# Which engine makes the low halves of the weights, and how a row of token factors is spread over the partitions

## The chip, the core and the metric

The kernel runs on one core of a Trainium2 chip. The metric is the device time of one execution in microseconds (us), the median of several runs. The engines are TensorE (PE, its weight loads shown apart as PEld), VectorE (DVE), ScalarE (ACT), GpSimd (POOL) and SyncE (SP, which issues most DMAs).

## What is computed

A decoder trunk of two layers on 512 tokens of width 1024, in float32. The first layer mixes with a gated delta rule (8 heads of 128), the second with forgetting attention (16 heads of 64). Each layer then has a gated feed-forward part (SwiGLU, inner width 2816).

```python
def swiglu(h, w_in, w_out):
    gu = h @ w_in
    return (jax.nn.silu(gu[..., :D_FF]) * gu[..., D_FF:]) @ w_out
...
    for layer in range(DEPTH):
        h = rms_norm(x, pre_mix_norm[layer])
        ...
        x = x + rms_norm(mix, post_mix_norm[layer])
        f = swiglu(rms_norm(x, pre_ffn_norm[layer]), w_ffn_in[layer], w_ffn_out[layer])
        x = x + rms_norm(f, post_ffn_norm[layer])
    return x
```

`mix` is the delta rule, or attention on shared keys and values. `rms_norm` divides each token by the root of the mean of its squares, so every norm needs one factor per token.

## The kernel before, in words

**Tiling.** The residual is kept transposed: features on the partitions, 8 tiles of 128 features, 512 tokens along the free dimension. A unit of weights is 128 output features by 1024 input features.

**Split products.** To keep float32 accuracy, every weight and every activation is split into a high half (rounded to fp32r) and a low half (the remainder). A product takes three passes per block of 128 inputs: high by high, low by high, high by low (`product`). A unit therefore costs 24 passes of 512 columns on PE. Its halves are made by `halve`: ACT copies the loaded tile `wf` into `wh`, then DVE or POOL subtracts, `wl = wf - wh`. Each of `wf`, `wh` and `wl` has four buffers.

**Who subtracts.** `next_halves` decides for each unit, from the planner's clocks: `late` is how far DVE's planned work reaches beyond PE's present time. In the kernel before, POOL gets the unit when `late` is over 1.0 us and either the unit is not yet wanted or POOL would be done sooner.

**The order of the work.** Nothing runs while the program text is executed: the calls on `PE`, `DVE`, `ACT`, `POOL` and `SP` are recorded with a planned cost (`Plan.cost`, `Plan.note`), by generators (`main`, `gates`, `k_post`, `inverse`, `recurrence`, `boundary`, ...) that a small planner resumes. Afterwards `ordered` and `listed` make four rounds of list scheduling over all recorded groups and keep the best. Each engine then executes its own list strictly in that order. So a decision in one place can move instructions everywhere; in the trace all recorded instructions bear the line of the recording helper (L102), and tiles tell them apart.

**Stages.** First come the normalised input (tiles `b`) and the units of k and z. Beside them, `gates` makes the decay matrices: a series on 32 columns (tiles `sp`) on DVE, then per head two products with `SLR` into bank `mid` and an exponential on ACT. `k_post` (per head: three convolution steps on DVE, SiLU on ACT, column sums into bank `sm`, four 128x128 products into `mid`) leads to the head's matrix; `inverse` inverts all of them in 31 steps on DVE; `merge` and `recurrence` follow. Then out projection, the first boundary, the feed-forward part, the second boundary, attention, the third boundary, the second feed-forward part, and the finish.

**A boundary** (`boundary`, `first_units`, `token_rsqrt`) leads from one sublayer to the next, in two halves of 256 tokens. The output tiles are scaled (tiles `b`), added to the residual (tiles `a`, three of four on POOL), and split into the next operand (tiles `h`: high by ACT, low by DVE) for eight feature tiles in turn. PE's first products of the next sublayer, into banks `ob` and `prj`, take one feature tile after the other as they come.

**The token factor** (`token_rsqrt`, lines 712 to 726) sums squares over features by products with a column of ones into `sm` (128 tokens per column), DVE scales them (`tokr`), POOL raises them to the power -1/2 (`tokn`, `tokp`), and for each chunk of 128 tokens a product of the broadcast column with the identity puts the row of factors on all partitions, in bank `mid`. There are 15 such calls with 32 chunks: one of four chunks at the start, and 14 of two chunks.

Of the kernel before, what the change touches and what calls it, by code (L numbers as in the profile page):

```python
# [17 lines left out]
P = 128  # L18
# [406 lines left out]
def trunk(  # L425
# [21 lines left out]
    plan = Plan()  # L447
    PE, DVE, ACT, POOL, SP = (
        plan.engine(e, n)
        for e, n in ((nc.tensor, "PE"), (nc.vector, "DVE"), (nc.scalar, "ACT"), (nc.gpsimd, "POOL"), (nc.sync, "SP"))  # L450
    )
# [35 lines left out]
    def small(shape, tag, bufs, dt=F32):  # L487
        return plan.tile(tag, bufs, spool, shape, dt, nm(tag))
# [7 lines left out]
    def mid():  # L496
        return bank("mid", 2)

    def sm():
        return bank("sm", 2)  # L500
# [7 lines left out]
    def ck(c, n=P):  # L508
        return slice(c * n, (c + 1) * n)
# [3 lines left out]
    ident, U = (cst_sb[:, i] for i in range(2))  # L513
# [28 lines left out]
    def signal(name, after=0.0):  # L542
        signals[name] = max(plan.now(), current[0][5], plan.finish)
# [51 lines left out]
    used = [0]  # L595
# [11 lines left out]
    def halve(pieces=1, act=ACT, dve=None):  # L607
        i = len(ready)
        _, n, eng, cols, thin = seq[i]
        t = landed[i]  # L610
        hi = plan.tile("wh", 4, wpool, [P, KT, P], F32R, nm("wh"))
        if not thin:
            lo = plan.tile("wl", 4, wpool, [P, KT, P], F32R, nm("wl"))
            ready.append((hi[:, :, :cols], lo[:, :, :cols]))
        else:

            lo = hi[:, :, cols:]
            ready.append(hi[:, :, : 2 * cols])
        landed[i] = None
        left[i] = n * T  # L620
        index[hi.tensor.name] = i
        step = n // pieces

        def piece(k):
            a, h, l = (w[:, k : k + step, :cols] for w in (t, hi, lo))
            act.activation(h, a, AF.Copy)
            (dve or eng).tensor_tensor(out=l, in0=a, in1=f(h), op=ALU.subtract)

        return [lambda k=k: piece(k) for k in range(0, n, step)]
# [3 lines left out]
    def landing():  # L633
        while len(landed) < min(used[0] + 5, len(ready) + 4, len(seq)):
            for go in land():
                go()

    def next_halves():

        i = len(ready)  # L640
        landing()
        late = plan.free["DVE"] - plan.now()
        slow = late > 1.0 and (used[0] < i or late + 1.2 > 2.4 + plan.free["POOL"] - plan.now())
        for go in halve(dve=POOL if slow else DVE):
            go()
        landing()
        signal(f"half{i}")

    def halver():
        while len(ready) < len(seq):  # L650
            i = len(ready)
            if i > 3:
                yield (f"left{i - 4}",)
            yield (lambda: 0.0 if used[0] >= i else min(plan.free["DVE"], plan.free["POOL"]) - 0.4,)
            if len(ready) == i:
                next_halves()
# [4 lines left out]
    def unit():  # L661
        i = used[0]
        used[0] += 1
        while len(ready) <= i:
            next_halves()
        landing()
        return ready[i]
# [40 lines left out]
    def token_sums(ps, src, chunks):  # L708
        for c in chunks:
            PE.matmul(ps[:, c : c + 1], lhsT=src[:, ck(c)], rhs=ones[:, 0:1], start=True, stop=True)  # L710

    def token_rsqrt(acc, tok, r, use):

        cs = range(tok.start // P, tok.stop // P)
        sl = slice(cs[0], cs[-1] + 1)
        yield ("#sm", plan.ready(acc[:, tok]))
        ps = sm()
        token_sums(ps, acc, cs)
        m = small([P, NC], "tokr", 4)
        DVE.tensor_scalar(out=m[:, sl], in0=ps[:, sl], scalar1=1.0 / D, scalar2=EPS, op0=ALU.mult, op1=ALU.add)  # L720
        POOL.tensor_tensor(out=r[:, sl], in0=m[:, sl], in1=mhalf[:, sl], op=ALU.pow)
        yield ("done", "#mid")
        ps = mid()
        for c in cs:
            PE.matmul(ps[:, ck(c)], lhsT=r[:, c : c + 1].broadcast_to([P, P]), rhs=ident, start=True, stop=True)
        use(ps[:, tok])

    def halves_of(x, k, sets, hs, tok, act=ACT, dve=DVE):
# [5 lines left out]
    class Norm:  # L734
# [7 lines left out]
        def factor(self, i, tok):  # L742
            def use(ps):
                ACT.activation(self.rs[:, tok], ps, AF.Copy)

            yield from token_rsqrt(self.acc, tok, self.r, use)
            signal(f"{self.name}.rs{i}")

    def finish(x, mix, acc, g, tok):

        r = small([P, NC], "tokp", 2)
        banks = []
        yield from token_rsqrt(acc, tok, r, banks.append)
        for k in range(KT):
            m, xk = mix[k][:, tok], x[k][:, tok]
            DVE.scalar_tensor_tensor(out=m, in0=m, scalar=gain(g, k), in1=banks[0], op0=ALU.mult, op1=ALU.mult)
            (POOL if k % 2 else DVE).tensor_tensor(out=xk, in0=m, in1=xk, op=ALU.add)
            SP.dma_start(out=out[:, k, tok], in_=xk)

    def boundary(i, x, mix, acc, g, norm):  # L760

        tok = HALF[i]
        r = small([P, NC], "tokp", 2)
        banks = []
        yield from token_rsqrt(acc, tok, r, banks.append)
        plan.hold(banks[0])
        for k in range(KT + 1):
            yield (calm(),)
            if k < KT:
                m, xk = mix[k][:, tok], x[k][:, tok]  # L770
                DVE.scalar_tensor_tensor(out=m, in0=m, scalar=gain(g, k), in1=banks[0], op0=ALU.mult, op1=ALU.mult)
                (POOL if k % 4 else DVE).tensor_tensor(out=xk, in0=m, in1=xk, op=ALU.add)
            if k > 0:
                halves_of(x, k - 1, norm.sets[:1], norm.h[:1], tok, ACT, DVE)
                signal(f"{norm.name}.h{i}.{k - 1}", 0.5)
        plan.hold(banks[0], False)
        if i == 1:
            for j in range(2):
                spawn(statistics(j, x, norm), -2)
# [946 lines left out]
```

## Time and profile before

| what | value |
|---|---|
| median of 3 runs | 1376.98 us (1375.44 to 1379.12) |
| the profiled execution, its own time | 1375.52 us |
| its span, from the first to the last instruction | 1373.8 us |
| mean granted TensorE clock | 0.985 |
| busy: PE, PEld | 1338.3 us (97%), 1120.5 us (82%) |
| busy: DVE, ACT, POOL | 800.6 us (58%), 587.4 us (43%), 260.8 us (19%) |
| DMA | 115.14 MB, mean 84 GB/s |

Busy time is the time in which an engine had an instruction under way; a waiting engine is not busy. Matmuls overlap, so PE at 97% does not say that it ran at full rate in that time. The granted clock says at which share of 2.4 GHz PE was allowed to run: the records show only 1.0 and 0.5 (1.2 GHz).

### The profile page before, as it was taken

The numbers are of one execution on the slowest core, as the hardware profiler recorded it, in microseconds if no ns is written. First come the engines' busy times: TensorE is split into PE (matmuls) and PEld (weight loads), VectorE is DVE, ScalarE is ACT, GpSimd is POOL, SyncE is SP. The second block draws the span as 40 slices with busy tenths as digits, with TensorE's granted clock in tenths as the row PEclk, the third lists the DMA queues.
The fourth block names the chain that finished last, engine by engine and source line by source line (L and its number), as shares of the span: only waits on it lengthen the run. The fifth ranks groups of instructions, "written<-read, shape, count | busy, mean of one in ns | idle before, by whom it ended". The sixth has DMA issues, their size and how long they took to land.

```text
span 1373.8 us, 18683 instructions
## 1 busy us (share of the span) xinstructions
PE 1338.3 (97%) x7374; PEld 1120.5 (82%) x7374; DVE 800.6 (58%) x1323; ACT 587.4 (43%) x1106; POOL 260.8 (19%) x168
## 2 busy tenths in 40 slices
PE   7999999999999999999999999999999999999996
PEld 5878887888988888888889787777988888888886
DVE  6968886555874443234558668586685443224455
ACT  5465345455552322222326557575554232222231
POOL 2423100321510000002235441210440000002222
PEclk9989999999999999999999999999999999999998
DMA  6211310112323223333321422110323323333311
GB/s 218 87 32 62 108 62 31 47 47 85 101 95 106 92 86 90 112 96 106 94 93 46 118 84 65 62 47 2 105 73 103 104 89 92 96 108 92 105 49 62
DMA packets 37687, 115.14 MB, mean 84 GB/s; under 512 B 6448, under 2 KB 8752, under 8 KB 37600
## 3 DMA queue, kind: packets, MB, share of 16 engines
q1 hardware_dynamic: 35728, 111.43, 26.1%
q10 hardware_dynamic: 1872, 2.53, 0.6%
q8 instruction: 58, 0.95, 0.3%
q14 instruction: 29, 0.24, 0.1%
HBM read 111.78 MB, written 2.16 MB: 83 GB/s over the span
## 4 chain that ended last, share of the span: by engine, by line
PE 92%; DVE 3%; ACT 2%; POOL 1%; DMA 1%; issue 1%; SPq 0%; POOLq 0%; ACTq 0%; DVEq 0%
PE prj L102 78%; PE mid L102 5%; PE sm L102 5%; PE ob L102 4%; DVE b L102 1%; DVE w L102 1%; ACT b L102 1%; DMA cst_sb<-in_cst_dram 0%; DVE a L102 0%; POOL wl L102 0%; ACT w L102 0%; ACT wh L102 0%; DMA wf<-in_w_gdn_dram 0%; DVE h L102 0%; POOL a L102 0%
## 5 line engine op out<-in xcount | busy, mean ns | idle before, releaser
L102 PE MATMUL prj<-h,wh 128*128 128x512 f32 (+1 forms) x1968 | 616.2, 386 | 1.5 <-DVE a L102 0.8
L102 PEld LDWEIGHTS prj<-h,wh 128*128 128x128 f32 x1968 | 369.5, 190 | 70.4 <-ACT w L102 1.5
L102 ACT ACTIVATE wh<-wf 128x1024 fp32r<-128x1024 f32 (+2 forms) x211 | 217.2, 1032 | 488.3 <-PE prj L102 270.9
L102 PE MATMUL prj<-b,wh 128*128 128x512 f32 (+3 forms) x1408 | 405.4, 367 | 4.5 <-DVE b L102 3.6
L102 PE MATMUL prj<-h,wl 128*128 128x512 f32 (+1 forms) x984 | 375.5, 382 | 0.6 <-POOL wl L102 0.6
L102 POOL TENSOR_TENSOR wl<-wf,wh 128x1024 fp32r<-128x1024 f32 x72 | 181.2, 2520 | 862.1 <-ACT wh L102 842.7
L102 PEld LDWEIGHTS prj<-b,wh 128*128 128x128 f32 (+2 forms) x1408 | 250.6, 187 | 49.1 <-DVE b L102 5.1
L102 DVE TENSOR_TENSOR wl<-wf,wh 128x1024 fp32r<-128x1024 f32 (+2 forms) x138 | 168.7, 1224 | 161.4 <-ACT wh L102 161.3
L102 PE MATMUL prj<-b,wl 128*128 128x512 f32 (+2 forms) x696 | 251.5, 361 | 0.4 <-DVE wl L102 0.4
L102 PEld LDWEIGHTS prj<-h,wl 128*128 128x128 f32 x984 | 187.2, 190 | 32.6 <-POOL wl L102 1.0
L102 DVE TENSOR_TENSOR w<-prj,w 128x512 f32<-128x512 f32 (+2 forms) x92 | 63.2, 690 | 186.4 <-PE prj L102 186.3
L102 PEld LDWEIGHTS prj<-b,wl 128*128 128x128 f32 (+1 forms) x696 | 131.2, 188 | 19.2 <-DVE wl L102 1.0
L102 DVE TENSOR_TENSOR w<-w,w 128x256 f32<-128x256 f32 (+1 forms) x133 | 103.0, 781 | 33.3 <-ACT w L102 27.4
L102 DVE TENSOR_TENSOR b<-w,b 128x512 fp32r<-128x512 f32 (+1 forms) x60 | 68.3, 1142 | 13.8 <-ACT b L102 13.4
L102 ACT ACTIVATE b<-w 64x512 fp32r<-64x512 f32 (+1 forms) x92 | 57.4, 630 | 20.4 <-DVE w L102 19.6
L102 ACT ACTIVATE b<-sm,m 128x512 f32<-128x512 f32 (+3 forms) x64 | 33.4, 524 | 29.4 <-DVE m L102 29.0
L102 PE MATMUL prj<-wh,b 128*128 128x512 f32 x128 | 44.6, 404 | 0.0
L102 POOL TENSOR_TENSOR a<-b,a 128x256 f32<-128x256 f32 x44 | 38.3, 879 | 28.6 <-DVE b L102 28.5
L102 DVE TENSOR_REDUCE m<-sm 128x1 f32<-128x512 f32 (+3 forms) x64 | 30.6, 486 | 15.1 <-PE sm L102 14.9
L102 ACT ACTIVATE b<-prj 128x512 f32<-128x512 f32 (+1 forms) x53 | 28.7, 542 | 24.2 <-PE prj L102 24.2
L102 ACT ACTIVATE b<-mid 128x512 f32<-128x512 f32 (+6 forms) x53 | 24.4, 462 | 26.4 <-PE mid L102 26.0
L102 DVE SCALAR_TENSOR_TENSOR h<-a,gains_sb,h 128x256 fp32r<-128x256 f32 x48 | 34.9, 744 | 0.2 <-ACT h L102 0.2
(185 smaller groups left out, 1319.6 us busy)
## 6 DMA issues: line engine op xcount, KB each, us to landing
wf<-in_w_ffn_in_dram SPq DMA_DIRECT2D x88, 512.0 KB
wf<-in_w_ffn_out_dram SPq DMA_DIRECT2D x32, 512.0 KB
wf<-in_w_gdn_dram SPq DMA_DIRECT2D x31, 512.0 KB
wf<-in_w_ffn_out_dram SPq DMA_DIRECT2D x16, 384.0 KB
wf<-in_w_gdn_out_dram SPq DMA_DIRECT2D x8, 512.0 KB
wf<-in_w_q_dram SPq DMA_DIRECT2D x8, 512.0 KB
wf<-in_w_k_dram SPq DMA_DIRECT2D x8, 512.0 KB
wf<-in_w_v_dram SPq DMA_DIRECT2D x8, 512.0 KB
```

The costliest lines, as they stand in the source:

```text
L102: self.call(*[real(v) for v in self.args], **{k: real(v) for k, v in self.kw.items()})
```

## The change

Two places. In `next_halves` POOL gets a unit only if DVE's planned work reaches over 4.0 us beyond PE's present time and the unit is not yet wanted; in all other cases DVE gets it. In `token_rsqrt` the product of the broadcast column with the identity becomes a transpose of the broadcast column by the same identity, with the same operands and the same result.

```diff
@@ next_halves
         late = plan.free["DVE"] - plan.now()
-        slow = late > 1.0 and (used[0] < i or late + 1.2 > 2.4 + plan.free["POOL"] - plan.now())
+        slow = late > 4.0 and used[0] < i
         for go in halve(dve=POOL if slow else DVE):
             go()
@@ token_rsqrt
         ps = mid()
         for c in cs:
-            PE.matmul(ps[:, ck(c)], lhsT=r[:, c : c + 1].broadcast_to([P, P]), rhs=ident, start=True, stop=True)
+            PE.transpose(ps[:, ck(c)], r[:, c : c + 1].broadcast_to([P, P]), ident)
         use(ps[:, tok])
```

The program before has 72 subtractions `wl<-wf,wh` on POOL, the changed one 14. Of the 58 that move to DVE, 21 stood ahead of the end of the first boundary, 23 in the two feed-forward parts, the others at the second and third boundary and beside attention. The planner's clocks move with them, so the lists of all engines are laid out anew. Three places follow, with the buffer numbers as each program has them.

The first is DVE's list at the start, where `b` are the low halves of the normalised input, `w_157` and `w_124` the running sum of squares, and `negb` and `identb` casts of constants that ACT's queue loads. Before:

```order
L102 TENSOR_TENSOR wl_159<-wf_118,wh_145 128x8x16
L102 CAST negb<-w_136 128x128
L102 TENSOR_TENSOR w_157<-w_157,w_149 128x512
L102 SCALAR_TENSOR_TENSOR b_169<-a_121,gains_sb,b_169 128x512
L102 TENSOR_TENSOR w_157<-w_157,w_172 128x512
L102 SCALAR_TENSOR_TENSOR b_178<-a_127,gains_sb,b_178 128x512
```

Changed:

```order
L102 SCALAR_TENSOR_TENSOR b_202<-a_140,gains_sb,b_202 128x512
L102 SCALAR_TENSOR_TENSOR b_212<-a_148,gains_sb,b_212 128x512
L102 TENSOR_TENSOR w_124<-w_124,w_226 128x512
L102 SCALAR_TENSOR_TENSOR b_218<-a_153,gains_sb,b_218 128x512
L102 CAST identb<-cst_sb 128x128
L102 TENSOR_SCALAR tokr_260<-sm_238 128x4
L102 CAST negb<-w_117 128x128
```

The cast `negb` stood ahead of the fourth `b`; now it stands behind the eighth and last one, and behind `tokr`.

The second is PE's list where the decay matrices are done and the products of `k_post` begin (`mid<-b` 128x128, `sm<-ones,a`). Before:

```order
L102 MATMUL prj_700<-h_569,wh_538 128x512
L102 MATMUL mid_756<-b_349 128x128 x4
L102 MATMUL sm_768<-ones,a_761 128x1 x4
L102 MATMUL mid_779<-b_349 128x128 x4
L102 MATMUL mid_791<-b_423 128x128 x3
L102 MATMUL sm_797<-ones,a_783 128x1 x4
L102 MATMUL sm_806<-ones,a_795 128x1 x4
L102 MATMUL mid_791<-b_423 128x128
L102 MATMUL prj_819<-h_341,wh_581 128x512
```

Changed:

```order
L102 MATMUL prj_682<-b_218,wh_501 128x512
L102 MATMUL mid_722<-b_343 128x128 x4
L102 MATMUL prj_731<-h_322,wh_553 128x512
L102 MATMUL prj_731<-h_322,wl_645 128x512
L102 MATMUL prj_731<-h_322,wh_553 128x512
L102 MATMUL prj_731<-h_359,wh_553 128x512
L102 MATMUL prj_731<-h_359,wl_645 128x512
L102 MATMUL prj_731<-h_359,wh_553 128x512
L102 MATMUL sm_745<-ones,a_736 128x1 x4
L102 MATMUL sm_753<-ones,a_743 128x1 x4
```

Before, 24 of the 64 such products stood together, three projections (`prj`) behind the last product with `SLR`; now 45 projections stand between that one and the first of them, and they come in fours and eights with 3 to 12 projections between.

The third is DVE's list in the first half of the first boundary (`w_3256`, `w_3258`: sum of squares of the half to come). Before:

```order
L102 TENSOR_TENSOR wl_3496<-wf_3297,wh_3465 128x1024
L102 TENSOR_TENSOR w_3256<-w_3256,w_3504 128x256
L102 SCALAR_TENSOR_TENSOR h_3488<-a_3220,gains_sb,h_3488 128x256
L102 SCALAR_TENSOR_TENSOR b_3302<-b_3302,gains_sb,mid_3456 128x256
L102 SCALAR_TENSOR_TENSOR h_3498<-a_3227,gains_sb,h_3498 128x256
L102 TENSOR_TENSOR w_3256<-w_3256,w_3541 128x256
L102 SCALAR_TENSOR_TENSOR b_3302<-b_3302,gains_sb,mid_3456 128x256
L102 SCALAR_TENSOR_TENSOR h_3567<-a_3234,gains_sb,h_3567 128x256
```

Changed:

```order
L102 TENSOR_TENSOR wl_3491<-wf_3294,wh_3468 128x1024
L102 SCALAR_TENSOR_TENSOR h_3486<-a_3222,gains_sb,h_3486 128x256
L102 TENSOR_TENSOR w_3258<-w_3258,w_3503 128x256
L102 SCALAR_TENSOR_TENSOR b_3306<-b_3306,gains_sb,mid_3458 128x256
L102 TENSOR_TENSOR wl_3534<-wf_3323,wh_3511 128x1024
L102 TENSOR_TENSOR w_3258<-w_3258,w_3543 128x256
L102 SCALAR_TENSOR_TENSOR h_3524<-a_3229,gains_sb,h_3524 128x256
```

One subtraction more stands on DVE between the first `h` and the second; the two that POOL had between its additions `a` of this half are gone from POOL's list. The third boundary reads the same. At the second, POOL had two as well, and now two subtractions stand on DVE ahead of the first `h`.

## Rows read from the trace of the kernel before

**Rows 1.** The page: busy time of the engines, and the chain by engine.
```profile
PE 1338.3 (97%) x7374; PEld 1120.5 (82%) x7374; DVE 800.6 (58%) x1323; ACT 587.4 (43%) x1106; POOL 260.8 (19%) x168
...
PE 92%; DVE 3%; ACT 2%; POOL 1%; DMA 1%; issue 1%; SPq 0%; POOLq 0%; ACTq 0%; DVEq 0%
```

**Rows 2.** Stretches of 50 us: busy PE, PEld, DVE, ACT, POOL, granted clock, DMA share, GB/s.
```profile
50.00:100.00 50.00, 47.74 (x210) 39.31 (x209) 38.41 (x50) 26.56 (x51) 18.57 (x8) 0.87 0.20 62
100.00:150.00 50.00, 48.02 (x242) 40.95 (x241) 40.37 (x89) 23.68 (x53) 10.33 (x7) 0.96 0.23 74
...
650.00:700.00 50.00, 50.00 (x222) 41.42 (x221) 24.34 (x22) 14.69 (x18) 12.44 (x5) 1.00 0.31 95
...
900.00:950.00 50.00, 50.00 (x384) 37.95 (x384) 41.72 (x106) 38.47 (x101) 5.08 (x2) 1.00 0.08 23
```

**Rows 3.** Waits of PE: who ended them, us in total, times, longest.
```profile
PE ob L102 <- DVE h L102: 4.6, 3, 1.8
PE mid L102 <- ACT b L102: 3.8, 2, 2.3
...
PE prj L102 <- DVE b L102: 3.6, 2, 1.9
```

**Rows 4.** The stretches of half clock, columns as in rows 2.
```profile
86.80:100.50 13.70, 13.70 (x57) 12.83 (x57) 7.37 (x19) 10.65 (x27) 4.42 (x3) 0.50 0.01 1
110.70:114.10 3.40, 3.40 (x11) 2.82 (x11) 3.18 (x8) 3.21 (x11) 1.01 (x1) 0.50 0.02 5
...
366.70:370.10 3.40, 3.40 (x16) 3.40 (x17) 3.18 (x8) 1.72 (x4) 2.65 (x4) 0.50 0.54 159
998.20:1001.60 3.40, 3.25 (x16) 3.19 (x16) 3.40 (x8) 1.70 (x5) 2.25 (x4) 0.50 0.33 134
```

**Rows 5.** Timeline of the start: start, us, instruction, [idle before it <- who ended it].
```profile
12.20 0.23 DVE L102 CAST negb<-w 128x128 bf16<-128x128 f32 x1 [2.90 <-DMA w<-in_cst_dram]
...
16.86 2.85 DVE L102 SCALAR_TENSOR_TENSOR b<-a,gains_sb,b 128x512 fp32r<-128x512 f32 x1
...
16.31 2.86 POOL L102 TENSOR_TENSOR wl<-wf,wh 128x1024 fp32r<-128x1024 f32 x1 [15.87 <-ACT wh L102]
...
33.17 0.42 PE L102 MATMUL sm<-cst_sb,w 16*128 16x16 f32 x4 [2.15 <-DVE w L102]
```

**Rows 6.** Timeline of the gates and of the first products of `k_post`.
```profile
40.78 0.18 DVE L102 SCALAR_TENSOR_TENSOR sp<-sp,sp 128x32 f32<-128x32 f32 x1
...
41.54 2.43 DVE L102 SCALAR_TENSOR_TENSOR sp<-sp,sp 128x32 f32<-128x32 f32 x1
...
41.16 2.76 POOL L102 TENSOR_TENSOR wl<-wf,wh 128x1024 fp32r<-128x1024 f32 x1 [12.59 <-ACT wh L102]
...
85.72 1.16 PE L102 MATMUL mid<-b 128*128 128x128 f32 x8 [2.26 <-ACT b L102]
```

**Rows 7.** Timeline of the first boundary, DVE and POOL.
```profile
359.81 0.48 DVE L102 SCALAR_TENSOR_TENSOR h<-a,gains_sb,h 128x256 fp32r<-128x256 f32 x1
...
364.38 2.19 DVE L102 SCALAR_TENSOR_TENSOR h<-a,gains_sb,h 128x256 fp32r<-128x256 f32 x1
...
363.75 2.54 POOL L102 TENSOR_TENSOR wl<-wf,wh 128x1024 fp32r<-128x1024 f32 x1
```

**Rows 8.** Groups by form, whole span: xcount | busy us, mean ns | idle before <- releaser.
```profile
L102 POOL TENSOR_TENSOR wl<-wf,wh 128x1024 fp32r<-128x1024 f32 x72 | 181.2, 2520 | 862.1 <-ACT wh L102 842.7
L102 DVE TENSOR_TENSOR wl<-wf,wh 128x1024 fp32r<-128x1024 f32 x119 | 151.8, 1277 | 129.8 <-ACT wh L102 129.7
```

**Rows 9.** Groups by form on DVE, first from 400 to 600 us, then from 600 to 700.
```profile
L102 DVE TENSOR_TENSOR b<-w,b 128x512 fp32r<-128x512 f32 x14 | 9.5, 684 | 0.0
...
L102 DVE TENSOR_TENSOR b<-w,b 128x512 fp32r<-128x512 f32 x8 | 17.0, 2123 | 5.6 <-ACT b L102 5.6
```

**Rows 10.** Timeline: four passes of two products of the token factor, four transposes of attention.
```profile
355.48 0.60 PE L102 MATMUL mid<-cst_sb,tokp 128*128 128x128 f32 x4
...
903.12 0.60 PE L102 MATMUL mid<-cst_sb,b 128*128 128x128 f32 x4
```

## The prediction

> **What bounds the kernel now.** I read the page first: PE is busy 97% of the span, and 92% of the chain that ended last is PE [rows 1]. So time is saved only where PE waits, where it runs at half clock, or where it has passes to do that can go. The stretches of 50 us show where that is: from 650 to 700 us PE is busy 50.00 of 50.00 at clock 1.00 although POOL works 12.44 us beside it, while from 50 to 150 us it loses 4.2 us of busy time and the clock falls to 0.87 and 0.96 [rows 2]. The waits of PE name three causes of size: `h` from DVE (4.6 us, three times), `b` from ACT (3.8), `b` from DVE (3.6) [rows 3]. The half-clock stretches add to that: 13.7 and 3.4 us near the gates, 3.4 us at the first and at the third boundary [rows 4]; each costs half its length.
>
> Next, why ACT and DVE are late. Twice the same pattern: a step on 32 columns takes 0.18 us, and 2.43 us when it is issued while POOL subtracts; POOL's subtraction ends at 43.92 us and the step at 43.97 [rows 6]. At the boundary a low half `h` takes 0.48 us and 2.19 us, again ending with POOL's subtraction [rows 7]. In the feed-forward part the same subtraction `b<-w,b` takes 684 ns on average in a stretch without POOL and 2123 ns in one with it [rows 9]. So a DVE operation on two tiles in SBUF stands still while POOL subtracts. A unit on POOL takes 2.52 us, on DVE 1.28 us [rows 8]: where it hits, POOL's help costs DVE some 1.4 to 2.2 us to spare it 1.28.
>
> **The change, part by part.** All sums are against the profiled execution, 1375.52 us; the median of the runs is 1.5 us above it.
>
> *Transposes.* 32 products have two passes each; four passes (two products) take 0.60 us, and four transposes of the same shape 0.60 us as well [rows 10]. A pass started every (0.60 - 0.27) / 3 = 0.11 us, if the last is under way 0.27 us. One pass of two goes: 32 x 0.11 = 3.5 us of PE. Nothing covers PE, so I take 3.5; the low end is 0, if every one falls in a wait.
>
> *Start.* DVE stood 2.90 us before the cast `negb`, whose constants had not landed, ahead of the fourth `b`; the sixth `b` took 2.85 us while POOL subtracted; and PE waited 2.15 us for the gate logits, behind a token factor that queued on POOL [rows 5]. The new order has `negb` behind the last `b`, POOL's first unit comes after ACT has made all `b`, and 15 projections stand between factor and logits. PE's waits here are 3.6 [rows 3] + 2.15 = 5.7 us. But the sums of squares stand further forward now and need all eight squares, so PE may wait there for up to the 2.85 us of one such stall. Ends: 5.7 won, 2.85 lost; I take 4 won, since each cause seen is gone from its place.
>
> *Gates and `k_post`.* Of nine units that POOL had up to 80 us, seven go to DVE, at 1.28 us each; the stalls of some 2.2 us each go from a series of dependent steps. The decay matrices stand some 45 passes earlier in PE's list, and 45 projections now cover ACT's table load and SiLU, for which PE waited 2.26 us [rows 6]. The waits are 3.8 us [rows 3]. The clock fell right behind that wait, in the block of 24 small products that the new order spreads; the two stretches cost (13.7 + 3.4) / 2 = 8.5 us [rows 4]. Ends: 12.3 won; 2.3 lost, if another wait like that one appears. I take 8, the waits and half of the clock, nearer the upper end because both the wait and the block are gone from the list.
>
> *Inverse, merge and recurrence.* In the 31 steps DVE has nine units instead of seven, POOL one instead of four or so: 2 x 1.28 added, 3 stalls of up to 2.2 removed, 4 us shorter. PE has 12 projections fewer to cover them, 12 x 0.225 (50.00 / 222 [rows 2]) = 2.7 us. Close to level: I take 0, between -3 and +3.
>
> *Boundaries.* At the first and third, the two POOL units between the additions go and one more DVE unit comes: two stalls of 1.7 us (2.19 - 0.48) against 1.28. PE's waits were 4.6 us, the longest (1.8) at the second boundary; so 2.8 at the two, and half of 2 x 3.4 for the clock: 6.2 us. At the second boundary two DVE units stand ahead of the first `h` where two stalls were: 0. Ends: 6.2 won; 3 x 1.28 = 3.8 lost, if every new unit falls on the path. I take 5, because the stalls go from the very operations that PE waited for.
>
> *Steady feed-forward.* 23 units move beside a full PE: 0. Their cover is DVE's room: 24.34 of 50 busy, and five more units are 6.4 us. Without that room they would be late by 1.28 us each.
>
> *What is late next.* A unit on POOL that waits for ACT's `wh` holds up nobody; on DVE it holds up all behind it. DVE's units waited 129.7 / 119 = 1.1 us each for `wh` [rows 8]. 21 moved ahead of the end of the first boundary: 0 to 23 us, of which I charge 4, since DVE has 10 us of room per 50 there [rows 2].
>
> Sum: 3.5 + 4 + 8 + 0 + 5 - 4 = 16.5 us. 1375.5 - 16.5 = 1359.0, with the 1.5 us to the median 1360.5; I say **1360 us**.
>
> The page "TensorE: Matmul & The Clock Gate" of the Trainium skill, section "Part 4: PE-mode transpose", says that transposes do not count as PE activity for the clock; by it the new token factors could pull the clock down. It is the fifth case below.
>
> **The rivals.** 1. *My forecast:* 1360.
>
> 2. *Half the waits go, the clock stays.* The stretches follow wherever small products are dense, waits or not. For it: the clock fell within products of few columns [rows 6]. Against: from 900 to 950 us PE does 384 such and larger passes at 1.00 without a wait [rows 2]. Won: 3.5 + half of 5.7, 3.8 and 2.8, less 2 for new waits = 7.7; 1367.8 + 1.5 = 1369.
>
> 3. *The change doesn't do what it says for PE: the inverse on DVE sets the pace.* Then what start and gates win is waited for again at the merge. For it: DVE is busy 40.37 of 50 there [rows 2]. Against: the inverse starts when the last head's matrix is there, which comes earlier by the same amount. Left: 3.5 + 5 - 4 = 4.5; 1371 + 1.5 = 1372.5, at the edge of no change.
>
> 4. *Slower: units stand in DVE's queue waiting for `wh`.* The place is DVE up to the first boundary, the price 1.28 + 1.1 = 2.4 us for a unit on the path. It overtakes the gains (20.5 us without the 4) from the ninth of 21 on; at 13 it gives 1375.5 - 20.5 + 31 + 1.5 = 1387. For it: DVE keeps strict order and is nearly full here. Against: POOL's stalls, which cost DVE as much, go.
>
> 5. *The clock falls at the token factors.* A stretch of 3.4 us costs 1.7; at all 15 calls 25.5 us, 1360.5 + 25.5 = 1386. Against: four transposes at 903 us lie in a stretch at 1.00 [rows 2, 10]. [...]
>
> **How the numbers follow.** Under about 0.3%, 4 us, a measurement of this kernel can't be told from no change. Chances: forecast 0.55, case 2 0.22, case 3 0.10 (0.03 of it faster, 0.07 same), case 4 0.10, case 5 0.03. Faster 0.55 + 0.22 + 0.03 = 0.80, same 0.07, slower 0.13. All upper ends won, with 3 from the recurrence, are 3.5 + 5.7 + 12.3 + 6.2 + 3 = 30.7, which gives 1346; case 3 with its own spread ends at 1375. The range 1346 to 1375 leaves out cases 4 and 5.
>
> **What would show it.** Right: POOL about 58 subtractions fewer; DVE's busy time no higher than before, since 58 x 1.28 = 74 us come and the stalls go; 32 passes into `mid` from `tokn` and `tokp` instead of 64; no wait of 2 us ahead of the first `mid<-b`; less than 10 us of half clock up to 130 us; no half clock at the first and third boundary; the feed-forward stretches unchanged at 222 passes per 50 us. Wrong: DVE waiting for ACT's `wh` with PE waiting for DVE behind it, a new wait of PE before the merge, or half-clock stretches right behind the token factors.

## The result and the profile after

The changed kernel takes **1355.8 us** in the median of 4 runs (1354.17 to 1357.55), beside 1377.84 us for the kernel before on the same chip: a ratio of 0.9842, 95% interval 0.982 to 0.9865. The forecast was 1360 us. The profiled execution has a span of 1352.4 us at a mean granted clock of 0.993, before it was 1373.8 at 0.985. Its first rows, which answer to [rows 1]:

```profile
PE 1325.8 (98%) x7342; PEld 1107.6 (82%) x7342; DVE 779.3 (58%) x1383; ACT 586.3 (43%) x1106; POOL 112.6 (8%) x109
...
PE 92%; DVE 4%; ACT 2%; issue 1%; DMA 0%; ACTq 0%; POOLq 0%; POOL 0%; DVEq 0%
```

PE's idle time, span less busy time, falls from 35.5 to 26.6 us. DVE has 60 instructions more and is busy 21.3 us less; POOL falls from 260.8 to 112.6. PE has 32 passes fewer.

Stretches of 50 us (the same columns as [rows 2]), the waits of PE as in [rows 3], and the stretches of half clock as in [rows 4]; apart from the tail these three are all that are left:

```profile
0.00:50.00 50.00, 47.26 (x212) 35.78 (x213) 41.28 (x80) 28.90 (x47) 6.40 (x7) 1.00 0.53 178
50.00:100.00 50.00, 50.00 (x280) 41.99 (x279) 38.43 (x76) 35.54 (x76) 9.74 (x7) 1.00 0.17 54
100.00:150.00 50.00, 50.00 (x234) 41.77 (x234) 44.06 (x89) 22.34 (x38) 3.83 (x3) 1.00 0.33 106
...
600.00:650.00 50.00, 50.00 (x222) 41.43 (x221) 23.27 (x28) 14.81 (x18) 0.00 (x0) 1.00 0.31 99
```

```profile
PE sm L102 <- DVE w L102: 4.5, 3, 2.2
PE prj L102 <- DVE a L102: 2.6, 2, 2.5
...
PE ob L102 <- DVE h L102: 0.9, 2, 0.4
...
PE prj L102 <- DVE b L102: 0.2, 1, 0.2
```

```profile
199.90:203.30 3.40, 3.40 (x12) 2.83 (x11) 1.24 (x5) 0.54 (x1) 1.26 (x2) 0.50 0.00 0
254.50:257.90 3.40, 3.40 (x14) 2.91 (x12) 1.47 (x3) 1.91 (x7) 0.00 (x0) 0.50 0.00 0
715.30:718.70 3.40, 3.40 (x18) 3.40 (x17) 3.31 (x8) 3.40 (x10) 1.57 (x2) 0.50 0.01 2
```

From 50 to 150 us PE now loses neither busy time nor clock; before, it lost 4.2 us there and ran at 0.87 and 0.96. The wait for ACT's `b` [rows 3] is gone. The feed-forward part still does 222 passes in 50 us, with POOL idle.

The groups that answer to [rows 8] (whole span) and [rows 9] (DVE, 600 to 700 us), and the token factor of [rows 10]:

```profile
L102 DVE TENSOR_TENSOR wl<-wf,wh 128x1024 fp32r<-128x1024 f32 x177 | 216.5, 1224 | 134.7 <-ACT wh L102 134.2
...
L102 POOL TENSOR_TENSOR wl<-wf,wh 128x1024 fp32r<-128x1024 f32 x14 | 34.1, 2439 | 206.5 <-ACT wh L102 179.5 <-DVE m L102 20.7 <-PE sm L102 6.4
```

```profile
L102 DVE TENSOR_TENSOR b<-w,b 128x512 fp32r<-128x512 f32 x7 | 4.8, 684 | 0.0
```

```profile
20.96 0.60 PE L102 MATMUL mid<-cst_sb,tokn 128*128 128x128 f32 x4
```

58 units have left POOL, `b<-w,b` is back to 684 ns where it took 2123, and a whole token factor of four columns now takes the 0.60 us that two products took.

**Where the time came from.** The waits are those that the waits view lists; each stands in the stage of the pass that waited, in both traces. The clock is half the length of the half-clock stretches. Before minus after, us, won as plus:

| stage (in the trace of before) | waits of PE | clock |
|---|---|---|
| start, to 34 us | 8.0 - 2.7 = 5.3 | 1.7 |
| gates and `k_post`, 34 to 120 | 4.2 - 0 = 4.2 | 8.5 |
| inverse, merge, recurrence, to 330 | 4.8 - 6.4 = -1.6 | 0 |
| first boundary, to 405 | 2.0 - 1.4 = 0.6 | 1.7 |
| first feed-forward part | 0 | 0 |
| second boundary, 700 to 810 | 1.8 - 2.2 = -0.4 | -1.7 |
| attention | 1.2 - 0.9 = 0.3 | 0 |
| third boundary, 950 to 1050 | 0.8 | 1.7 |
| tail | -0.1 | -1.0 |

That is 9.1 of waits and 10.9 of clock, 20.0 of the 21.4 us that the span fell. The remaining 1.4 us are less than the 32 passes saved should give (3.5 [rows 10]); what took the rest is not shown.

### The profile page after: what moved, and what is told of

Its sections match the earlier page's. It is cut to its first block, busy times and chain, and to the rows that moved or that the text cites. A ratio compares the mean times of both kernels' runs of the same rounds, so it can differ in the third digit from the quotient of the medians.

```text
span 1352.4 us, 18625 instructions
## 1 busy us (share of the span) xinstructions
PE 1325.8 (98%) x7342; PEld 1107.6 (82%) x7342; DVE 779.3 (58%) x1383; ACT 586.3 (43%) x1106; POOL 112.6 (8%) x109
## 4 chain that ended last, share of the span: by engine, by line
PE 92%; DVE 4%; ACT 2%; issue 1%; DMA 0%; ACTq 0%; POOLq 0%; POOL 0%; DVEq 0%
PE prj L102 80%; PE mid L102 4%; PE sm L102 4%; PE ob L102 4%; DVE b L102 1%; ACT b L102 1%; DVE w L102 1%; DVE a L102 1%; ACT wh L102 0%; DMA gains_sb<-in_gains_dram 0%; DVE h L102 0%; ACT w L102 0%; DVE m L102 0%; DVE wl L102 0%; ACT a L102 0%
## 5 line engine op out<-in xcount | busy, mean ns | idle before, releaser
L102 PE MATMUL prj<-h,wh 128*128 128x512 f32 (+1 forms) x1952 | 607.9, 384 | 4.7 <-DVE a L102 2.5
L102 PEld LDWEIGHTS prj<-h,wh 128*128 128x128 f32 x1952 | 365.1, 189 | 72.3 <-issue 4.0
L102 PE MATMUL prj<-b,wh 128*128 128x512 f32 (+2 forms) x1424 | 411.5, 367 | 1.2 <-ACT wh L102 0.5
L102 PE MATMUL prj<-h,wl 128*128 128x512 f32 (+1 forms) x976 | 371.4, 380 | 0.0
L102 DVE TENSOR_TENSOR wl<-wf,wh 128x1024 fp32r<-128x1024 f32 (+1 forms) x196 | 233.5, 1192 | 166.3 <-ACT wh L102 165.8
L102 PEld LDWEIGHTS prj<-b,wh 128*128 128x128 f32 (+1 forms) x1424 | 253.2, 187 | 46.7 <-DVE b L102 2.5
L102 DVE TENSOR_TENSOR w<-w,w 128x256 f32<-128x256 f32 (+1 forms) x133 | 78.5, 597 | 24.3 <-ACT w L102 18.6
L102 POOL TENSOR_TENSOR tokp<-tokr,mhalf 128x2 f32<-128x2 f32 x8 | 6.1, 762 | 682.8 <-DVE tokr L102 682.8
L102 POOL TENSOR_TENSOR wl<-wf,wh 128x1024 fp32r<-128x1024 f32 x14 | 34.1, 2439 | 206.5 <-ACT wh L102 179.5
L102 DVE TENSOR_TENSOR b<-w,b 128x512 fp32r<-128x512 f32 (+1 forms) x60 | 41.5, 696 | 1.3 <-ACT b L102 1.0
L102 DVE TENSOR_REDUCE m<-sm 128x1 f32<-128x512 f32 (+3 forms) x64 | 30.4, 486 | 13.0 <-PE sm L102 12.7
L102 ACT ACTIVATE b<-mid 128x512 f32<-128x512 f32 (+6 forms) x53 | 24.6, 464 | 17.7 <-PE mid L102 17.3
```

Of the source, the lines that this page charges most:

```text
L102: self.call(*[real(v) for v in self.args], **{k: real(v) for k, v in self.kw.items()})
```

## The experiments

Two theories. **A**, that of the prediction: a DVE operation on two tiles in SBUF stalls while POOL subtracts, PE waits for the stalled results, and the clock falls behind the waits. **B**: the rule makes the planner lay other lists, and it is the place of PE's passes in them that saves the time, whichever engine subtracts.

**1. Each half of the change alone.** The first kernel has only the `PE.transpose` line of the diff, the second only the `slow` line.

> The transposes with the old rule for the units. Theory A (my sum): 32 passes go, 3.5 us, and the waits and half-clock stretches stay, so 1377.8 - 3.5 = 1374, between 1371 and 1377 since the lists shift a little. Rival (the removed passes fall in waits or the second pass costs nothing): 1377 to 1379. Rival (the products are what pulls the clock down near the gates): the stretches of 13.7 and 3.4 us go and it is 1366 or less.

> The new rule with the float32 products. Theory A: the whole gain less the 3.5 us of passes, 1355.8 + 3.5 = 1359 (1357 to 1362), with no half clock before the merge. Rival (the two parts need each other, because the lists of the whole change come only with both): 1365 or more.

Measured: transposes alone 1374.16 us (ratio 0.9969, 0.9958 to 0.9981), the rule alone 1362.08 (0.989, 0.9873 to 0.9907). Gains of 3.1 and 15.1 us beside 1377.23 for the kernel before. The transposes are worth what the passes cost, and with them alone the half clock near the gates stays (10.2 us from 99.3 on), so the products did not bring it. The rule alone is 3 us above the expected 1359, at the edge of its range, and the expected "no half clock before the merge" missed: its lists have 6.8 us of half clock at the start and as much at 173 and at 221 us. The parts add up to 18.2 of the 22.0 us between the medians, and each new laying has other small losses.

**2. Lists and engines exchanged.** All lists stay; only the engine that issues a subtraction is another. `MOVED` are the 62 units that only the old rule puts on POOL (the old rule has 73 with the thin one, 11 of them are among the new rule's 14).

```diff
             for item in group.items:
+                if item.op == "tensor_tensor" and item.outs[0].tensor.tag in ("wl", "wh") and item.ins[0].tensor.tag == "wf":
+                    if item.ins[0].tensor.index in MOVED:
+                        item.call = nc.gpsimd.tensor_tensor
                 item.issue()
```

In the kernel before, the same edit has `nc.vector`.

> The changed kernel, every engine's list as it is, but the 62 subtractions that the old rule alone had on POOL are issued on POOL at the same place of the program. Theory A (DVE's stalls behind POOL make PE late): the stalls are back at the start, the gates and the boundaries, 1.4 to 2.2 us each, and with them waits of PE and half-clock stretches: 10 to 20 us slower than the changed kernel, 1366 to 1376. Theory B (the new order of the passes does it, and the engine of the units matters little): at most 3 us slower, 1356 to 1359.

> The kernel before, every engine's list as it is, but the same 62 subtractions are issued on DVE at the same place of the program. Theory A: the stalls go, the waits for late constants and for the token factor stay, so 6 to 12 us faster than before, 1366 to 1372. Theory B: no gain, or a loss because units now stand in DVE's strict list at places that were chosen for POOL, 1376 to 1385.

Measured: new lists with the old engines **1359.91 us** (0.9873, 0.986 to 0.9886), old lists with the new engines **1374.96** (0.9988, 0.9979 to 0.9997). Both lie nearer to what B expected, though neither in its range: the first is 0.9 us above it, the second between the two ranges. The first kernel has POOL as busy as before (267.6 us) and the stalls back:

```profile
L102 DVE TENSOR_TENSOR b<-w,b 128x512 fp32r<-128x512 f32 x44 | 52.7, 1202 | 11.2 <-ACT b L102 11.2
```

(684 ns each in the changed kernel), and yet at the gates PE loses only 1.1 us and no clock:

```profile
50.00:100.00 50.00, 48.88 (x271) 40.71 (x270) 40.01 (x69) 33.56 (x70) 20.09 (x11) 1.00 0.17 54
100.00:150.00 50.00, 50.00 (x236) 41.82 (x235) 45.93 (x86) 21.06 (x38) 13.35 (x7) 1.00 0.33 104
```

The second has DVE's stalls gone. At the start and the gates PE's waits are as large as before [rows 3] or larger; those for `h` at the boundaries fall from 4.6 to 2.1 us:

```profile
PE prj L102 <- DVE b L102: 4.7, 2, 2.6
PE mid L102 <- ACT b L102: 4.2, 3, 2.3
PE sm L102 <- DVE w L102: 4.2, 3, 2.2
PE ob L102 <- DVE h L102: 2.1, 3, 0.9
```

So the stalls are worth some 4 us with the new lists and 2 with the old ones; the lists carry the rest.

By place the two runs say more. A kernel and its exchanged partner have the same list on PE, so the n-th pass of one trace can be held beside the n-th of the other. With the old lists the engines alone won 2.4 us at the first boundary and 2.7 at the third, where the waits for `h` fell from 1.4 to 0.6 us each and the half clock went; they won 2.7 in `k_post`, where the first wait stayed but the half clock near the gates fell from 17.1 to 10.2 us. They lost 3.1 ahead of it and 3.8 near 300 us (a wait for `rhs` of 1.75 us instead of 0.61, and 6.8 us of half clock from 299.3 on). With the new lists the stalls cost nothing at the start, 1.4 us ahead of `k_post` and 1.3 to 1.5 at each boundary. These are single traces, and starts with the same lists differ by up to 1.9 us (experiment 5), so the loss ahead of `k_post` may be scatter. A holds at the boundaries, where PE waits for the stalled operation itself.

The wait of 2.26 us ahead of `k_post` has the same length in both kernels with the old lists. ACT's timeline shows why: from PE's last product with `SLR` on, ACT makes the exponentials, loads a table and makes the SiLU, and the critical path through this wait holds no operation of DVE. First in the kernel before, then with the engines exchanged, 3.06 us later:

```profile
81.42 0.60 ACT L102 ACTIVATE b<-mid 128x512 f32<-128x512 f32 x1 [3.52 <-PE mid L102]
...
83.75 1.28 ACT L102 ACT_TABLE_LOAD   x1
85.04 0.63 ACT L102 ACTIVATE b<-b 128x512 f32<-128x512 f32 x1
...
86.81 1.28 ACT L102 ACT_TABLE_LOAD   x1
88.79 1.16 PE L102 MATMUL mid<-b 128*128 128x128 f32 x8 [2.26 <-ACT b L102]
```

**3. The new rule for half of the program.** Up to unit 46 (the first boundary) one rule, behind it the other; with the transposes.

```diff
-        slow = late > 4.0 and used[0] < i
+        slow = late > 4.0 and used[0] < i if i <= 46 else late > 1.0 and (used[0] < i or late + 1.2 > 2.4 + plan.free["POOL"] - plan.now())
```

> The changed kernel with the new rule for the units up to the first boundary (1 to 46) and the old rule for all behind it, the planner laying all lists anew. Theory B (the gain lies in the lists up to the merge, as the runs with lists and engines exchanged suggest): nearly all is kept, 1358 to 1362, half clock only behind the second boundary and at the end. Theory A (stalls at every place cost): the boundaries and attention lose their part, 1364 to 1368.

> The other half: the old rule up to unit 46, the new one behind. Theory B: little is left over the transposes alone (1374.2), so 1368 to 1373, with the waits near 11, 18, 30 us and half clock at the gates as in the kernel before. Theory A: some 5 to 6 us better than the transposes alone, 1366 to 1369.

Measured: new rule early 1355.65 us (0.9841, 0.9806 to 0.9876), new rule late 1371.78 (0.9959, 0.9941 to 0.9976). The early half has the whole gain. It keeps 51 whole units on POOL, among them those of the feed-forward parts, so what moved there cost and gave nothing. With it alone the third boundary has losses again (one wait of 2.0 us for `tokp`, and 3.4 us of half clock from 981.1):

```profile
PE mid L102 <- POOL tokp L102: 3.1, 2, 2.0
```

Those losses are some 3 us and do not show in the medians, which are no finer.

**4. PE's list at the gates, packed.** The changed kernel; 16 groups of three projection passes that stand between the small products of `k_post` are issued ahead of the first of them. Nothing else moves.

```diff
-        for group in ordered(plan.items)[0]:
+        for group in packed(ordered(plan.items)[0]):
...
+        if kind(g) and kind(g)[0] == "prj":
+            count += 1
+            if all(o in done for o in g.before):
+                later.remove(g)
+                out.append(g)
```

> The changed kernel, only PE's list edited at one place: 48 projection passes that stand between the small products of k_post (72 to 90 us) are issued ahead of the first of them, so that the small products stand together, as before the change; every other engine's list stays. Theory (a dense block of small products brings the clock down, and PE waits inside it for the links of the chain): 7 to 14 us of half clock come back between 80 and 115 us, and 2 to 5 us of waits: 5 to 12 us slower than the changed kernel, 1361 to 1368. Rival (where the passes stand is indifferent as long as all engines do the same): at most 2 us slower, 1354 to 1358.

Measured: **1362.51 us** (0.9888, 0.9861 to 0.9916), 6.7 us slower than the changed kernel. One stretch of half clock is back, and PE loses 0.57 us of busy time in it:

```profile
86.70:103.80 17.10, 16.53 (x70) 15.71 (x71) 14.42 (x34) 14.71 (x40) 7.38 (x6) 0.50 0.14 38
```

What PE did before the clock fell, from its timeline:

```profile
82.55 0.39 PE L102 MATMUL prj<-h,wh 128*128 128x512 f32 x1
82.78 1.05 PE L102 MATMUL mid<-b 128*128 128x128 f32 x8
83.67 1.84 PE L102 MATMUL sm<-ones,a 128*128 128x1 f32 x16
85.38 1.14 PE L102 MATMUL mid<-b 128*128 128x128 f32 x8
```

There is no wait in front: full projections run up to 82.78, and the clock falls at 86.7 within small products. That is half of 17.1, 8.5 us, from the order of PE's passes alone, the same engines doing the same work. The traces agree on the place: before the gates the packed kernel is 0.2 us behind the changed one, behind them 9.0, and 8.6 at the end.

**5. PE's list at the gates, spread in the kernel before.** The counterpart: 43 groups of projections (129 passes; the expectation's 72 is a miscount) go one by one ahead of small products, as far as their operands and banks allow, which is from the 25th small pass of the block on (a product has two passes). The expectation speaks of the gates alone, but the edit does not stop there: 18 groups go to the gates, and 25 among later small products, from 160 us on, in merge and recurrence.

```diff
-        for group in ordered(plan.items)[0]:
+        for group in packed(ordered(plan.items)[0]):
...
+    for g in small:
...
+            if h not in done and h not in MOVED and all(o in done for o in h.before):
...
+                out.remove(h)
+                out.insert(at, h)
```

> The kernel before (old rule, products, all units where they were), only PE's list edited at one place: 72 projection passes from behind k_post's dense block are issued between its small products, three at a time. Theory (the block's density makes the clock fall): most of the 13.7 us stretch near 87 us goes, while the wait of 2.3 us ahead of the block stays: 4 to 7 us faster than before, 1370 to 1373. Rival (the wait ahead of the block, or DVE's stalls, make the clock fall): the stretch stays and it is within 2 us of before.

Measured: **1381.97 us** (1.0038, 1.0024 to 1.0052), slower than before; the forecast of a gain missed. The timeline shows why the clock was not saved: the block's head, 24 small passes behind the wait, could not be broken up, and the clock fell 0.7 us after that wait ended.

```profile
87.62 1.52 PE L102 MATMUL mid<-b 128*128 128x128 f32 x8 [2.26 <-ACT b L102]
88.94 1.71 PE L102 MATMUL sm<-ones,a 128*128 128x1 f32 x8
90.51 2.05 PE L102 MATMUL mid<-b 128*128 128x128 f32 x8
...
105.42 2.08 PE L102 MATMUL mid<-b 128*128 128x128 f32 x8 [1.71 <-ACT b L102]
```

It came back at 95.1, where it took until 100.5 before, fell again behind the second wait, and in all the gates have 13.7 us of half clock for 17.1. Where the time was lost shows when the same passes are held side by side, each pair first in the kernel before, then spread:

```profile
167.50 0.60 PE L102 MATMUL mid<-cst_sb,a 128*128 128x128 f32 x4
168.87 0.60 PE L102 MATMUL mid<-cst_sb,a 128*128 128x128 f32 x4
...
261.79 0.39 PE L102 MATMUL ob<-S,b 128*128 128x128 f32 x2
267.47 0.39 PE L102 MATMUL ob<-S,b 128*128 128x128 f32 x2
```

The spread kernel was 1.9 us behind at the block's first product (87.62 beside 85.72 [rows 6]), out of the start, where the edit moves nothing. Behind the gates it was 1.4 behind: they gained some 0.5 us. In merge and recurrence, where the other 25 groups went, it fell to 5.7 behind at 262 us and to 8.4 near 310, with 6.8 us of half clock from 303.3 on. At the end it was 5.9 behind. So the loss did not arise at the gates, and the run does not test what spreading there alone is worth; that stays open.

Nor does a change between projections and small products cost time. The first projection behind small passes starts its successor after 0.32 us instead of 0.225 (50.00 / 222 [rows 2]), but the small passes give that back: from 97.06 to 97.97 two of them and three projections take 0.91 us, and 2 x 0.11 + 3 x 0.225 is 0.90.

```profile
97.06 0.28 PE L102 MATMUL sm<-ones,a 128*128 128x1 f32 x2
97.19 0.48 PE L102 MATMUL prj<-h,wh 128*128 128x512 f32 x1
...
97.97 0.72 PE L102 MATMUL sm<-ones,a 128*128 128x1 f32 x6
```

**6. Other layings: luck or the rule?** The planner's `SLACK` (0.1 us in both kernels) shifts all lists a little. Three kernels have it at 0.3, one has no unit on POOL with 0.1.

```diff
-SLACK = 0.1
+SLACK = 0.3
...
-        slow = late > 4.0 and used[0] < i
+        slow = False
```

> The changed kernel with the planner's SLACK of 0.3 us for 0.1: the same 14 units on POOL but for two, all lists laid anew. If the gain hangs on the rule, 1350 to 1358, near the changed kernel, and it may be a little faster. If it was the luck of one laying, the scatter of layings shows: 1360 or more.

> The old rule with the transposes and the planner's SLACK of 0.3 us for 0.1, all lists laid anew. If the rule carries the gain: near the transposes alone, 1368 to 1377, however it is laid. If any new laying can give it: 1365 or less.

> The changed kernel with no unit on POOL at all, all lists laid anew. If the last 14 units on POOL still help DVE where it is behind (start, attention): 3 to 8 us slower than the changed kernel, 1359 to 1364. If they are as useless as the 58: 1353 to 1357.

> No unit on POOL and the planner's SLACK at 0.3 us. If idle time and half clock of PE decide and the units on POOL are worth nothing: like the new rule with the same SLACK, 1343 to 1350. If that kernel owes its time to one lucky laying: 1352 to 1360.

| rule (all with transposes) | SLACK 0.1 | SLACK 0.3 |
|---|---|---|
| old | 1374.16 | 1372.42 (1367.53 to 1382.59, 10 runs) |
| new | 1355.8 | **1345.21** (ratio 0.9765, 0.9737 to 0.9792) |
| no unit on POOL | 1354.57 (1353.55 to 1363.5; 0.9852, 0.9825 to 0.988) | 1346.33 (0.9782, 0.9766 to 0.9799) |

Both layings of the old rule are near 1373, all four with few or no units on POOL at or below 1356. So it is the rule, and not one lucky laying; but a new laying is worth up to another 10 us, more than was expected (the new rule with 0.3 is 5 us below its range). Two layings of the old rule and four of the others were tried. The last 14 units on POOL are worth nothing that shows.

Two kernels beat both. The faster one, the new rule with SLACK 0.3, has a clock of 0.997 and no half clock ahead of its tail. Its PE is idle for 22.6 us. At the gates its small products stand in small groups among the projections, as in the changed kernel, and PE is full at full clock:

```profile
50.00:100.00 50.00, 50.00 (x269) 41.66 (x268) 40.46 (x71) 34.59 (x68) 7.99 (x6) 1.00 0.19 57
```

**One sum for these kernels.** PE's idle time (span less busy time) and the clock's loss, (1 - granted clock) x span, account for most of the differences of the profiled executions (the clock is given to 0.001, so its loss to some 0.7 us):

| kernel | span | PE idle | clock's loss | units on POOL |
|---|---|---|---|---|
| before | 1373.8 | 35.5 | 20.6 | 73 |
| after | 1352.4 | 26.6 | 9.5 | 14 |
| transposes alone | 1370.4 | 33.4 | 23.3 | 74 |
| rule alone | 1360.2 | 27.1 | 15.0 | 13 |
| new lists, old engines | 1356.9 | 31.6 | 6.8 | 76 |
| old lists, new engines | 1372.7 | 33.7 | 22.0 | 11 |
| gates packed | 1361.0 | 27.7 | 17.7 | 14 |
| gates spread | 1379.7 | 39.8 | 17.9 | 73 |
| new rule, SLACK 0.3 | 1343.4 | 22.6 | 4.0 | 14 |

Where lists and rule belong together, few units on POOL go with less idle time (22.6 to 27.7 us beside 33.4 to 39.8). The two kernels with lists and engines exchanged part the two: 11 units with 33.7 us idle, 76 units with 31.6. What remains beside idle time and clock lies between 1313.7 us (transposes alone, 4.0 less than before) and 1322.0 (gates spread); the 32 passes saved explain a part of that, and the rest is not explained here.

## Why the prediction was right, and where its reasons were not

**The sum.** 16.5 us were forecast and 21.4 measured between the profiled executions, and the time lies in the range. The terms:

- *Transposes*, 3.5: 3.4 us of span when alone. Right. The token factors did not touch the clock: the first lies in a stretch at 1.00 (20.96 us, four transposes between projections). The page "TensorE: Matmul & The Clock Gate" of the Trainium skill says in "Part 4: PE-mode transpose" that a transpose does not count as PE-busy in the same way for the clock; no run here has a long row of them, so none bears on it.
- *Start*, 4: 7.0, beyond the upper end of 5.7. The waits went nearly whole (5.3); left out of the term was the half clock from 15.1 us on, worth 1.7. The lists made this gain: with the stalls back under the new ones the start was as fast.
- *Gates and `k_post`*, 8: 12.7, just over the upper end of 12.3. The text took half of the clock's share; all of it went.
- *Inverse, merge, recurrence*, 0 within 3: 1.6 lost, the longest a wait of 2.5 us for DVE's `a` at 250.9 us. A unit stands on DVE right ahead of the convolution steps that make it (249.40, 1.22 us), but it is not the cause: in the run with new lists and old engines that unit is on POOL, and the wait is 2.43 us.
- *Boundaries*, 5: 2.7. The first gave 2.3 and the third 2.5, but the second lost 2.1, a wait of 2.2 for the running sum of squares and 3.4 us of half clock behind it; it was costed at 0.
- *Late next*, a charge of 4: it did not fall due; not even the 1.6 of the recurrence is shown to be of this kind. Rival 4 had no place to bite: DVE's whole units waited 134.2 us for `wh` instead of 129.7 [rows 8], nearly always with PE busy.
- *Steady feed-forward*, 0: right. 23 units moved and 222 passes per 50 us stayed.

That the sum came near is in part luck. Start and gates gave 7.7 us more than was taken for them, the charge of 4 was not due, and boundaries and recurrence gave 3.9 less. The terms as measured, with attention and tail, add up to 23.4, 2.0 more than the span fell; the difference is not explained.

**The step that failed** is the link from the stalls to PE's waits, at the start and the gates. The text said of the gates that "the stalls of some 2.2 us each go from a series of dependent steps". The stalls are real, and they went. But with the stalls put back under the new lists 17.3 of the 22.0 us stay (some 3 of them the passes saved), and with the stalls taken from the old lists 2.3 are won. The wait ahead of `k_post` hung on PE's own last product with `SLR` and on ACT's work behind it, not on a stalled operation. What the text gave as a second reason was the cause there: in PE's list 45 projections stand ahead of the first product of `k_post`, and the block of 24 small products is spread. That 15 projections between factor and logits and the later `negb` made the start's gain fits the lists, but was not tried place by place.

At the boundaries the text said "because the stalls go from the very operations that PE waited for". There the link held, as experiment 2 shows in both directions. What failed is the size: the new lists brought a wait and half clock at the second boundary that had been put at 0.

**Rival 2**, that half clock follows dense small products whether PE waits or not, was given less weight because of a stretch with 384 passes at full clock. Packing the gates shows that it holds there: no wait, 17.1 us of half clock. Its conclusion that the clock would stay was wrong for another reason: the rule's lists had the block spread.

**What stays open** is why the planner finds these lists only with few units on POOL. It reckons a unit on POOL at 2.43 us during which DVE may do nothing on two tiles in SBUF, and lays all lists around that; that this reckoning is the reason was not tried.

## What to carry to other kernels

Where a scheduler lays the lists, a change of engine has two effects, and they can be told apart: issue the same lists with the engines exchanged. Here the lists had some 14 of 21 us, the passes 3 and the freed engine 2 to 4. Before a stall is priced as the cause of a wait, follow the chain that ends the wait: where it holds the stalled operation itself, as at the boundaries, the engine counts; where it holds other work, as ahead of `k_post`, what counts is what stands in the waiting engine's list to cover it.

On PE, count idle time and lost clock together. Packed into a block, the small products cost half of a stretch of 17.1 us; with projections between them, as in the changed kernel, they cost no clock. When an edit of a list is meant for one place, see from the traces that it ends there, and hold the same passes side by side: the total alone does not say where experiment 5 lost its time.

## What had not been expected of the hardware

- The clock fell with and without a wait in front. In the packed kernel it fell after 4 us of small products at full rate. In the kernel with the transposes alone, 16 small passes behind a wait of 0.2 us, three projections and 32 more small passes left it at full; twelve projections, 16 small passes and a wait of 1.65 us later it fell at once (99.3 us):

```profile
92.71 0.47 PE L102 MATMUL mid<-b 128*128 128x128 f32 x2
...
95.76 1.05 PE L102 MATMUL mid<-b 128*128 128x128 f32 x8
96.65 0.95 PE L102 MATMUL sm<-ones,a 128*128 128x1 f32 x8
99.25 2.07 PE L102 MATMUL mid<-b 128*128 128x128 f32 x8 [1.65 <-ACT b L102]
```

- A DVE cast with a single input stalls behind POOL too: in the changed kernel `negb` takes 1.92 us and ends as POOL's subtraction does (16.78 + 2.83 = 19.61), while 0.16 us for `tokr`, read from a PSUM bank, passes in between. The Trainium skill, page "SBUF — State Buffer", section "SBUF: two separate sides", has a lock on a port pair for this, held for a whole instruction, against DVE in a two-port mode or with two inputs in SBUF; the cast has one input, so the page covers it if it ran in such a mode, which no row shows; that it ends with POOL's subtraction agrees. The runs with the exchanged engines show how little such stalls may cost in all.

```profile
17.69 0.16 DVE L102 TENSOR_SCALAR tokr<-sm 128x4 f32<-128x4 f32 x1 [0.35 <-PE sm L102]
17.77 1.92 DVE L102 CAST negb<-w 128x128 bf16<-128x128 f32 x1
```
